# Low halves of weights by a negated cast on ScalarE and an adding transfer, and block sums on VectorE, in a hybrid encoder layer

## The chip, the core and the metric

The kernel is one launch on one core of one Trainium2 chip. It is written in a tile framework: the program allots named tiles from pools, and a scheduler sets the order of each engine's instructions and puts semaphore waits where a tile is not yet written or not yet free. The metric is the device time in microseconds, the median of the runs. Lower is better.

The engines are TensorE (PE, matmuls, with weight loads shown apart as PEld), VectorE (DVE), ScalarE (ACT), GpSimd (POOL) and SyncE (SP). SP and POOL also issue the transfers (DMA); in the code `dma` goes to SP's queue and `gdma` to POOL's.

## The reference

One layer for 1024 prompt tokens and 32 sample tokens, so T = 1056 columns, with D = 1024 and a feed-forward width of 2816. Everything is float32. Cut to what matters here:

```python
h = rms_norm(x, g_pre_mix)
z = h @ w_in                                    # split into q, k, v, HGRN2 inputs, gates ga and gb
ya = sink_attention(...)                        # windowed attention, 16 heads
yb = rms_norm(hgrn2(...), g) * silu(ob)         # gated linear recurrence, 8 heads
mix = sigmoid(ga) * (ya @ w_br_a) + sigmoid(gb) * (yb @ w_br_b)
x = x + rms_norm(mix @ w_out, g_post_mix)
hf = rms_norm(x, g_pre_ffn)
a, u = split(hf @ w_up, 2)                      # two halves of 2816 columns
a = causal_conv3(concat(prev, a)) + b_conv
x = x + rms_norm((gelu(a) * u) @ w_down, g_post_ffn)
x = x + (pe @ w_ple) * sigmoid(x @ w_ple_gate)
```

The outputs are x of both groups, the last keys and values, the recurrence's state and the convolution's tail.

## The kernel before, in words

**Split products.** A float32 product is made of three matmuls on a reduced type (fp32r). Each operand is split into a high half, hi = cast(raw), and a low half, lo = raw - hi. `product` adds hi x hi, hi x lo and lo x hi; the weight's low half is read by the third matmul only (L202, in the up stage L1867).

**Plain weights.** `plan` lists the weight tiles (128 columns, 512 KB) in the order of use. `next_w` returns the next one and calls `load_next` for the two behind it. `load_next` takes a raw tile ("wr", 2 buffers, loaded from DRAM by SP) and two of the eight 4 KB slots of the pool "wb" for hi and lo. hi comes from ScalarE (L181) and lo from VectorE (L184). The plan's entries 26 to 41 (n_first is 22) are the 8 tiles of w_br_a and the 8 of w_br_b. In this branch stage each tile meets four groups of 264 columns. A block of 24 matmuls fills one of six accumulator banks ("mm"), VectorE combines it with a gate tile "ta" (4 buffers), and POOL's queue stores the result to the DRAM tile mx_d (L1381).

**The up products.** A unit u is 128 columns of a with the 128 columns of u that belong to them, and there are 22 units. A unit is computed by a scheme of seven products (as Strassen and Winograd have it) in place of eight: its weights are seen as 2 x 2 blocks a11, a12, a21, a22 of 128 x 512 numbers, and the seven weight parts are

- part 0: a11
- part 1: a11 + s1, with s1 = a21 + a22
- part 2: a12
- part 3: a21 + a11, part 4: s1, part 5: a22
- part 6: a12 + a11 + s1

`unit_parts` is a generator that makes one part at each step: a cast to hi on ScalarE (L1625), the subtraction for lo on VectorE (L1626), both into one slot of "wb" (tile "wt"). The four block sums (L1632, L1633, L1634, L1639) are made on VectorE for unit 0 and on GpSimd (POOL) for the others. Three of them overwrite raw blocks, and s1 has a tile of its own, "sa", in a slot of "wb" too. `prepare` calls the generator so that parts stand three products ahead of their use (AHEAD = 3), so that a unit's first parts are made while the unit ahead is computed. The raw tiles (two of 512 KB a unit, loaded by SP at L1615) lie in "wr" for even units and in "wx" for odd ones, and the loads of unit u + 1 are written into the code behind part 3 of unit u.

Unit 0 is split early, in the z products' stage (`early_parts`), and its parts pass through the DRAM tiles pw_d.

**What follows a product.** `up_unit` runs the seven products of a unit, 24 matmuls each (2 column halves x 4 row blocks x 3); products 0 to 6 go to three accumulator tiles X, Y, Z ("st", 3 buffers). `after` takes them out: product 0 by ScalarE's copy to s1c (L1876), product 1 by VectorE's U2 = s1c - Y (L1878); L1894 is the last product's. Product 3 writes into Y again, so it waits for U2. At the unit's end `ff_tail` does the convolution: ScalarE's first tap (L1814), VectorE's other two (L1815, L1816), the gelu, and the product with u. The scheduler puts these beside the next unit's products.

Of the kernel before, what the change touches and what calls it, by code (L numbers as in the profile page):

```python
# [10 lines left out]
F32 = mybir.dt.float32  # L11
# [3 lines left out]
ALU = mybir.AluOpType  # L15
AX = mybir.AxisListType

P = 128
# [41 lines left out]
def layer_kernel(  # L60
# [10 lines left out]
    wp = ctx.enter_context(tc.tile_pool(name="wp", bufs=1, side="left"))  # L71
# [6 lines left out]
    def nm(s):  # L78
        n_names[0] += 1
        return f"{s}_{n_names[0]}"  # L80
# [4 lines left out]
    dma, gdma = nc.sync.dma_start, nc.gpsimd.dma_start  # L85
    V, S, G, E = nc.vector, nc.scalar, nc.gpsimd, nc.tensor
# [50 lines left out]
    def rows_cols(src, r0, c, n, kt):  # L137
        return src[0, r0:r0 + kt * P, c:c + n].rearrange("(k p) c -> p k c", p=P), kt, n
# [15 lines left out]
    n_first = len(plan)  # L154
# [11 lines left out]
    raws, ready, used = [], [], [0]  # L166

    def load_raw(raw=None):
        src, kt, n = plan[len(raws)]
        raws.append(raw or wp.tile([P, kt, n], F32, tag="wr", name=nm("wr"), bufs=2))  # L170
        dma(raws[-1][:], src)

    def load_next():
        _, kt, n = plan[len(ready)]
        if len(raws) == len(ready):
            load_raw()
        raw = raws[len(ready)]
        hi = wp.tile([P, kt, n], F32R, tag="wb", name=nm("wh"), bufs=8)
        lo = wp.tile([P, kt, n], F32R, tag="wb", name=nm("wl"), bufs=8)
        if hi_on[0] == "act":  # L180
            S.copy(hi[:], raw[:])  # L181
        else:
            V.tensor_copy(hi[:], raw[:])
        V.tensor_tensor(lo[:], raw[:], hi[:].bitcast(F32), op=ALU.subtract)  # L184
        ready.append((hi, lo))

    hi_on = ["act"]

    def next_w(ahead=2):
        while len(ready) < min(limit[0], used[0] + 1 + ahead):  # L190
            load_next()
        used[0] += 1
        return ready[used[0] - 1]
# [44 lines left out]
    def tr_bank():  # L238
        return bank(pp, "tr", 2)
# [738 lines left out]
    with right("bp") as bp:  # L978
# [322 lines left out]
        def more():  # L1301
            limit[0] = n_mix
            load_next()
# [10 lines left out]
        for c in range(4, 8):  # L1314
            u = unit(gate_out(tb_d[c]))
# [7 lines left out]
    def page(pool, n, shape, name):  # L1323

        return pool.tile(shape, F32R, tag=f"pg{n}", name=nm(name))
# [282 lines left out]
    raw_w, ready_w = {}, []  # L1608

    def unit_raw(u):  # L1610
        pool, tag = (wp, "wr") if u % 2 == 0 else (fp, "wx")
        t = []
        for h in (0, DFF):
            t.append(pool.tile([P, KT, P], F32, tag=tag, name=nm("wu"), bufs=2))
            dma(t[-1][:], rows_cols(w_up, 0, h + u * P, P, KT)[0])  # L1615
        raw_w[u] = t

    def unit_parts(u, s1, place, out):

        f1, f2 = raw_w.pop(u)  # L1620
        a11, a12, a21, a22 = f1[:, 0:4, :], f1[:, 4:8, :], f2[:, 0:4, :], f2[:, 4:8, :]

        def parts(i, src):
            t = place(i)
            S.copy(t[:, 0], src)  # L1625
            V.tensor_tensor(t[:, 1], src, t[:, 0].bitcast(F32), op=ALU.subtract)  # L1626
            out(i, t)

        adder = V if u < 1 else G

        parts(0, a11)
        adder.tensor_tensor(s1, a21, a22, op=ALU.add)  # L1632
        adder.tensor_tensor(a21, a11, a21, op=ALU.add)  # L1633
        adder.tensor_tensor(a11, a11, s1, op=ALU.add)  # L1634
        yield
        parts(1, a11)
        yield
        parts(2, a12)
        adder.tensor_tensor(a12, a12, a11, op=ALU.add)  # L1639
        yield  # L1640
        for i, src in enumerate((a21, s1, a22, a12)):
            parts(3 + i, src)
            yield

# [3 lines left out]
    def early_parts():  # L1648

        rw = page(lq, 4, [P, 2, KT, P], "rw")  # L1650
        rs_ = page(lq, 5, [P, 2, 2, 512], "rs")
        bufs = [page(lq, 6 + i, [P, 2, 2, 4, P], "pw") for i in range(2)]
        raw_w[0] = [rw[:, i].bitcast(F32) for i in range(2)]
        for i in range(2):
            dma(raw_w[0][i], rows_cols(w_up, 0, DFF * i, P, KT)[0])
        for i in range(2):
            dma(rs_[:, i].bitcast(F32), rows_cols(w_ple, 0, 512 * i, 512, 2)[0])

        place = [bufs[0][:, 0], bufs[0][:, 1], bufs[1][:, 0]]

        def store(i, t):
            gdma(pw_d[i][:], t.rearrange("p a k c -> p (a k c)").bitcast(F32))

        yield from unit_parts(0, bufs[1][:, 1, 0].bitcast(F32), lambda i: place[i % 3], store)
        for i in range(2):
            src = rs_[:, i].rearrange("p k c -> p (k c)")
            hi, lo = (place[(7 + 2 * i + a) % 3].rearrange("p a k c -> p (a k c)") for a in range(2))
            S.copy(hi, src.bitcast(F32))
            gdma(pw_d[7 + 2 * i][:], hi.bitcast(F32))
            V.tensor_tensor(lo, src.bitcast(F32), hi.bitcast(F32), op=ALU.subtract)  # L1670
            gdma(pw_d[8 + 2 * i][:], lo.bitcast(F32))
            yield
# [14 lines left out]
    n_parts, gens = [7], {}  # L1687

    def prepare(n):

        while n_parts[0] < min(n + 1, 7 * NF):
            u, i = divmod(n_parts[0], 7)
            if i == 0:
                if u not in raw_w:
                    unit_raw(u)
                s1 = wp.tile([P, 4, P], F32, tag="wb", name=nm("sa"), bufs=8)[:]
                gens[u] = unit_parts(u, s1, part_tile, lambda i, t: ready_w.append(t))
            next(gens[u])
# [43 lines left out]
    t = tr_bank()  # L1742
# [401 lines left out]
```

## Time and profile before

| | |
|---|---|
| median of 3 runs | 2002.01 us (2001.38 to 2003.11) |
| profiled execution | 2002.58 us |
| its span, first to last instruction | 2000.8 us |
| granted TensorE clock | 1.000 |
| PE busy | 1984.3 us (99%) |
| VectorE busy | 1424.5 us (71%) |
| ScalarE busy | 965.4 us (48%) |
| GpSimd busy | 228.4 us (11%) |

Times in rows of the profile are microseconds from the span's start. A row of a timeline gives start, length, engine, line, operation, result and inputs, partitions x elements, how many run together (x3), and in brackets how long the engine had been idle and which instruction released it. A row of a group has the count, the busy sum and the mean in nanoseconds of one, and then the idle time ahead of the group, by what ended it. A row of transfers has the count, the size of one, and the time from issue to landing. The branch stage lies around 940 us; the up products run from 1183 to 1637 us.

### The profile page before, as it was taken

Reading aid. Unit: us, or ns where it says so; the run is one execution under the profiler, and the core shown is the slowest. Engines: PE = TensorE matmul, PEld = TensorE weight load, DVE = VectorE, ACT = ScalarE, POOL = GpSimd, SP = SyncE. Lnnn points to the kernel's source line nnn. Section 1 sums busy time; section 2 is a strip of 40 time slices with the busy share of each in tenths; the row PEclk is TensorE's granted clock in tenths of the full one; section 3 lists DMA queues with packets and bytes.
Section 4 is the critical chain, followed back from the end, with each engine's and each line's share of the span. In section 5 each row is a group of like instructions: output and inputs, shape, how many; then the busy total and the mean of one; then the engine's idle time right before and its main releaser. Section 6 shows DMA issues by size and latency. Waiting matters only on the chain.

```text
span 2000.8 us, 37359 instructions
## 1 busy us (share of the span) xinstructions
PE 1984.3 (99%) x14304; PEld 1955.0 (98%) x14304; DVE 1424.5 (71%) x3138; ACT 965.4 (48%) x2159; POOL 228.4 (11%) x323
## 2 busy tenths in 40 slices
PE   8999999999999999999999999999999999999998
PEld 7899999999999999999999999999999999999998
DVE  6788888688888888554455788788888784655552
ACT  7555566566666666442124663333333344444432
POOL 1110100000000000002001023333333210000000
PEclk9999999999999999999999999999999999999999
DMA  7622311411111111377558582222222245655543
GB/s 257 155 92 85 106 53 55 154 43 58 58 37 51 41 54 54 123 241 220 166 165 291 173 288 70 80 76 86 76 86 76 86 141 195 213 192 173 171 130 80
DMA packets 253639, 247.47 MB, mean 124 GB/s; under 512 B 13893, under 2 KB 221912, under 8 KB 253461
## 3 DMA queue, kind: packets, MB, share of 16 engines
q1 hardware_dynamic: 245141, 218.59, 35.3%
q0 software_dynamic: 8240, 26.44, 3.7%
q8 instruction: 112, 1.84, 0.4%
q14 instruction: 66, 0.54, 0.1%
q10 hardware_dynamic: 80, 0.07, 0.0%
HBM read 177.56 MB, written 65.32 MB: 121 GB/s over the span
## 4 chain that ended last, share of the span: by engine, by line
PE 92%; DVE 4%; ACT 2%; DMA 1%; issue 1%; POOL 0%; SPq 0%; DVEq 0%; ACTq 0%; POOLq 0%
PE mm L200 14%; PE mm L201 14%; PE mm L202 14%; PE st L1867 7%; PE st L1866 7%; PE st L1865 7%; PE G L1009 2%; PE Y L1006 2%; PE G L1008 2%; PE G L1006 2%; PE Y L1009 2%; PE Y L1008 2%; PE tr L478 1%; PE X L1006 1%; PE so L1200 1%; PE X L1009 1%
## 5 line engine op out<-in xcount | busy, mean ns | idle before, releaser
L1865 PE MATMUL st<-op,wt 128*128 128x264 f32 x1232 | 348.6, 283 | 2.0 <-DVE Sp L1878 1.3
L1867 PE MATMUL st<-op,wt 128*128 128x264 f32 x1232 | 349.8, 284 | 0.0
L1866 PE MATMUL st<-op,wt 128*128 128x264 f32 x1232 | 347.6, 282 | 0.0
L184 DVE TENSOR_TENSOR wl<-wr,wh 128x1024 fp32r<-128x1024 f32 x129 | 157.9, 1224 | 120.7 <-ACT wh L181 111.7
L1865 PEld LDWEIGHTS st<-op,wt 128*128 128x128 f32 x1232 | 231.2, 188 | 3.5 <-DVE Sp L1878 1.7
L1866 PEld LDWEIGHTS st<-op,wt 128*128 128x128 f32 x1232 | 231.4, 188 | 0.0
L1867 PEld LDWEIGHTS st<-op,wt 128*128 128x128 f32 x1232 | 230.9, 187 | 0.0
L181 ACT CAST wh<-wr 128x1024 fp32r<-128x1024 f32 x116 | 121.8, 1050 | 197.7 <-PE mm L201 136.1
L200 PE MATMUL mm<-La,wh 128*128 128x384 f32 (+1 forms) x528 | 174.4, 331 | 0.0
L201 PE MATMUL mm<-Lb,wh 128*128 128x384 f32 (+1 forms) x528 | 170.9, 324 | 0.6 <-DVE Lb L710 0.6
L200 PE MATMUL mm<-ac,wh 128*128 128x352 f32 x528 | 170.8, 323 | 0.0
L202 PE MATMUL mm<-La,wl 128*128 128x384 f32 (+1 forms) x528 | 170.5, 323 | 0.2 <-DVE wl L685 0.2
L202 PE MATMUL mm<-ac,wl 128*128 128x352 f32 x528 | 169.8, 322 | 0.0
L201 PE MATMUL mm<-ac,wh 128*128 128x352 f32 x528 | 169.3, 321 | 0.0
L1625 ACT CAST wt<-wu 128x512 fp32r<-128x512 f32 x126 | 77.9, 619 | 186.6 <-POOL ab L1851 88.3
L200 PE MATMUL mm<-Ra,wh 128*128 128x264 f32 x512 | 145.4, 284 | 0.0
L201 PE MATMUL mm<-Rb,wh 128*128 128x264 f32 x512 | 145.0, 283 | 0.0
L202 PE MATMUL mm<-Ra,wl 128*128 128x264 f32 x512 | 145.0, 283 | 0.0
L1626 DVE TENSOR_TENSOR wt<-wu,wt 128x512 fp32r<-128x512 f32 x126 | 103.0, 820 | 39.0 <-ACT wt L1625 39.0
L462 ACT ACTIVATE sc<-sc,st 128x257 f32<-128x257 f32 (+1 forms) x144 | 69.7, 485 | 74.0 <-DVE st L457 73.0
L201 PEld LDWEIGHTS mm<-Lb,wh 128*128 128x128 f32 x528 | 99.4, 188 | 1.7 <-DVE Lb L710 1.4
L202 PEld LDWEIGHTS mm<-La,wl 128*128 128x128 f32 x528 | 99.2, 188 | 0.7 <-DVE wl L685 0.5
(496 smaller groups left out, 5694.8 us busy)
## 6 DMA issues: line engine op xcount, KB each, us to landing
wr<-in_w_down_dram SPq DMA_DIRECT2D x66, 512.0 KB
wu<-in_w_up_dram SPq DMA_DIRECT2D x42, 512.0 KB
wu<-in_w_in_dram SPq DMA_DIRECT2D x32, 512.0 KB
wr<-in_w_in_dram SPq DMA_DIRECT2D x25, 512.0 KB
ac<-act_d SPq DMA_DIRECT2D x66, 176.0 KB
act_d<-Up SPq DMA_DIRECT2D x21, 528.0 KB
wr<-in_w_out_dram SPq DMA_DIRECT2D x16, 512.0 KB
pw_d<-pw POOLq DMA_DIRECT2D x11, 512.0 KB, 5.6
```

The source lines that it names most:

```text
L181: S.copy(hi[:], raw[:])
L184: V.tensor_tensor(lo[:], raw[:], hi[:].bitcast(F32), op=ALU.subtract)
L200: E.matmul(ps, wh, a, start=first and n == 0, stop=False)
L201: E.matmul(ps, wh, b, start=False, stop=False)
L202: E.matmul(ps, wl, a, start=False, stop=last and n == len(ks) - 1)
L1006: E.matmul(o, wh, x[0][k], start=first and k == 0, stop=False, skip_group_check=True)
L1008: E.matmul(o, wh, x[1][k], start=False, stop=False, skip_group_check=True)
L1009: E.matmul(o, wl, x[0][k], start=False, stop=k == 3, skip_group_check=True)
L1626: V.tensor_tensor(t[:, 1], src, t[:, 0].bitcast(F32), op=ALU.subtract)
L1865: E.matmul(o, wh, xh, start=first and k == 0, stop=False, skip_group_check=True)
L1866: E.matmul(o, wh, xl, start=False, stop=False, skip_group_check=True)
L1867: E.matmul(o, wl, xh, start=False, stop=k == 3, skip_group_check=True)
```

## The change

Three things change.

1. For the plan's entries 26 to 41 (the branch weights), lo is no longer made by VectorE. ScalarE writes -raw into the lo tile (a negated cast), and a transfer of GpSimd's queue adds raw to it.

2. The same for the seven parts of each unit from 1 on. Unit 0 keeps VectorE's subtraction.

3. The four block sums of every unit are made on VectorE, and a11 + s1 goes to a new second half of the tile "sa", where before it overwrote a11. The last sum now goes into a11.

As written, the result of the adding transfer is -cast(raw) + raw, since the tile that ScalarE writes holds the reduced type.

```diff
@@ load_next
+        if n_first + 4 <= len(ready) < n_first + 20:
             S.copy(hi[:], raw[:])
+            S.mul(lo[:], raw[:], -1.0)
+            gdma(lo[:], raw[:], accum_op=ALU.add)
         else:
-            V.tensor_copy(hi[:], raw[:])
-        V.tensor_tensor(lo[:], raw[:], hi[:].bitcast(F32), op=ALU.subtract)
+            if hi_on[0] == "act":
+                S.copy(hi[:], raw[:])
+            else:
+                V.tensor_copy(hi[:], raw[:])
+            V.tensor_tensor(lo[:], raw[:], hi[:].bitcast(F32), op=ALU.subtract)
@@ unit_parts
-    def unit_parts(u, s1, place, out):
+    def unit_parts(u, s1, s2, place, out):
...
             S.copy(t[:, 0], src)
-            V.tensor_tensor(t[:, 1], src, t[:, 0].bitcast(F32), op=ALU.subtract)
+            if u:
+                S.mul(t[:, 1], src, -1.0)
+                gdma(t[:, 1], src, accum_op=ALU.add)
+            else:
+                V.tensor_tensor(t[:, 1], src, t[:, 0].bitcast(F32), op=ALU.subtract)
             out(i, t)
 
-        adder = V if u < 1 else G
-
         parts(0, a11)
-        adder.tensor_tensor(s1, a21, a22, op=ALU.add)
-        adder.tensor_tensor(a21, a11, a21, op=ALU.add)
-        adder.tensor_tensor(a11, a11, s1, op=ALU.add)
+        V.tensor_tensor(s1, a21, a22, op=ALU.add)
+        V.tensor_tensor(a21, a11, a21, op=ALU.add)
+        V.tensor_tensor(s2, a11, s1, op=ALU.add)
         yield
-        parts(1, a11)
+        parts(1, s2)
         yield
         parts(2, a12)
-        adder.tensor_tensor(a12, a12, a11, op=ALU.add)
+        V.tensor_tensor(a11, a12, s2, op=ALU.add)
         yield
-        for i, src in enumerate((a21, s1, a22, a12)):
+        for i, src in enumerate((a21, s1, a22, a11)):
             parts(3 + i, src)
             yield
@@ prepare
-                s1 = wp.tile([P, 4, P], F32, tag="wb", name=nm("sa"), bufs=8)[:]
-                gens[u] = unit_parts(u, s1, part_tile, lambda i, t: ready_w.append(t))
+                sa = wp.tile([P, 2, 4, P], F32, tag="wb", name=nm("sa"), bufs=8)
+                gens[u] = unit_parts(u, sa[:, 0], sa[:, 1], part_tile, lambda i, t: ready_w.append(t))
```

`early_parts` passes the second half of its scratch tile for s2. Lines of the changed file lie 5 higher in its first part and 8 higher from the up products on: L1814, L1815, L1816, L1876, L1878 of before are L1822, L1823, L1824, L1884, L1886 after, and the sums are L1639, L1640, L1641, L1646.

The scheduler orders the changed program anew. The next rows are VectorE's, before, from the last product of one unit (L1894) to U2 of the next (L1878) in a steady stretch of the up stage. The number behind a tile's name tells which allotment it is; `st` are accumulators, `ab` the convolution's input, `a` its sum, `Sp` holds s1c and U2, and a wait on PE, Activation or DMAHW is one on TensorE, ScalarE or a transfer of SP's queue.

```order
L1894 TENSOR_TENSOR Sp_14910<-Sp_14910,st_15645 128x528 [waits PE_49]
L1626 TENSOR_TENSOR wt_15990<-wu_15876,wt_15990 128x512 [waits DMAHW4_49,Activation_49]
L1898 TENSOR_TENSOR ab_15646<-Sp_14910,rbT 128x2x232 [waits DVE_49]
L1901 TENSOR_TENSOR ab_15646<-Sp_14910,rbT 128x32 x2
L1810 COPY tails<-ab_15646 128x2 [waits DVE_49]
L1811 COPY tails<-ab_15646 128x2 [waits DVE_49]
L1813 COPY ab_15646<-cach 128x2
L1815 TENSOR_SCALAR a_15856<-ab_15646,cvec,a_15856 128x1058 [waits Activation_49]
L1816 TENSOR_SCALAR a_15856<-ab_15646,cvec,a_15856 128x1058 [waits DVE_49]
L1878 TENSOR_TENSOR Sp_14910<-Sp_14910,st_15869 128x528 [waits PE_49,Activation_49]
```

The same stretch after; DMASW is a transfer of GpSimd's queue.

```order
L1902 TENSOR_TENSOR Sp_14926<-Sp_14926,st_15910 128x528 [waits PE_49]
L1906 TENSOR_TENSOR ab_15911<-Sp_14926,rbT 128x2x232 [waits DVE_49]
L1909 TENSOR_TENSOR ab_15911<-Sp_14926,rbT 128x32 x2
L1818 COPY tails<-ab_15911 128x2 [waits DVE_49]
L1819 COPY tails<-ab_15911 128x2 [waits DVE_49]
L1821 COPY ab_15911<-cach 128x2
L1639 TENSOR_TENSOR sa_16265<-wu_16151 128x512 [waits DMASW6_49,DMAHW0_49,DMASW1_49,PE_49]
L1823 TENSOR_SCALAR a_16128<-ab_15911,cvec,a_16128 128x1058 [waits Activation_49]
L1640 TENSOR_TENSOR wu_16151<-wu_16149,wu_16151 128x512 [waits DMASW6_49,DMAHW7_49,DMASW2_49,DVE_49]
L1824 TENSOR_SCALAR a_16128<-ab_15911,cvec,a_16128 128x1058 [waits DVE_49]
L1886 TENSOR_TENSOR Sp_14926<-Sp_14926,st_16141 128x528 [waits PE_49,Activation_49]
```

The low half's subtraction is gone, and two block sums stand between, one ahead of the first convolution step and one between the two.

ScalarE in the same stretch before, from part 4's cast (of tile "sa") to the copy of s1c:

```order
L1625 COPY wt_16130<-sa_15989 128x512 [waits PE_49]
L1625 COPY wt_16158<-wu_15878 128x512 [waits DVE_49]
L1625 COPY wt_16186<-wu_15876 128x512 [waits PE_49,Pool_49]
L1625 COPY wt_16215<-wu_16101 128x512 [waits DMAHW7_49,PE_49]
L1814 ACTIVATE a_16081<-ab_15871,cvec 128x1058 [waits DVE_49]
L1876 COPY Sp_14910<-st_16093 128x528 [waits PE_49]
```

And after, where the ACTIVATE rows of L1632 are the negated casts:

```order
L1630 COPY wt_16178<-sa_16033 128x512 [waits PE_49]
L1632 ACTIVATE wt_16178<-sa_16033 128x512
L1630 COPY wt_16207<-wu_15919 128x512 [waits DMASW1_49,PE_49,Activation_49]
L1632 ACTIVATE wt_16207<-wu_15919 128x512
L1630 COPY wt_16236<-wu_15917 128x512 [waits DMASW4_49,DMASW7_49,DVE_49,Activation_49]
L1632 ACTIVATE wt_16236<-wu_15917 128x512
L1630 COPY wt_16266<-wu_16149 128x512 [waits DMAHW7_49,DMASW2_49,PE_49]
L1632 ACTIVATE wt_16266<-wu_16149 128x512
L1822 ACTIVATE a_16128<-ab_15911,cvec 128x1058 [waits DVE_49,Pool_49]
L1884 COPY Sp_14926<-st_16140 128x528 [waits PE_49]
```

Each part has a second operation on ScalarE, and part 6's cast (wt_16236) now waits for transfers of GpSimd's queue, where before it waited for PE and GpSimd. One of them, DMASW7, counts part 4's transfer out of the tile sa_16033, whose slot wt_16236 takes.

GpSimd in one unit before:

```order
L1632 TENSOR_TENSOR sa_15989<-wu_15878 128x512 [waits DMAHW5_49,DMAHW0_49,PE_49]
L1633 TENSOR_TENSOR wu_15878<-wu_15876,wu_15878 128x512 [waits DMAHW4_49,Pool_49]
L1634 TENSOR_TENSOR wu_15876<-wu_15876,sa_15989 128x512 [waits DVE_49,Pool_49]
L1851 MEMSET ab_16096 128x2 [waits DVE_49,Activation_49]
L1639 TENSOR_TENSOR wu_15876<-wu_15876 128x512 [waits DVE_49,Pool_49]
```

And after:

```order
L1633 DMA wt_16034<-wu_15917 128x512 [waits DMASW3_49,DMAHW4_49,PE_49,Activation_49]
L1859 MEMSET ab_16143 128x2 [waits DVE_49,Activation_49]
L1633 DMA wt_16066<-sa_16033 128x512 [waits DVE_49,DMASW4_49,PE_49,Activation_49]
L1633 DMA wt_16095<-wu_15917 128x512 [waits DMASW6_49,PE_49,Activation_49]
L1633 DMA wt_16145<-wu_15919 128x512 [waits DMASW7_49,DMAHW5_49,PE_49,Activation_49]
L1633 DMA wt_16178<-sa_16033 128x512 [waits PE_49,Activation_49]
L1633 DMA wt_16207<-wu_15919 128x512 [waits DMASW1_49,PE_49,Activation_49]
L1633 DMA wt_16236<-wu_15917 128x512 [waits DMASW4_49,DMASW7_49,DVE_49,Activation_49]
```

The sums have left the queue and seven adding transfers, one for each part, have come in.

More of the change, by code (lines that the diff above doesn't have):

```diff
@@ L179, in load_next @@
         lo = wp.tile([P, kt, n], F32R, tag="wb", name=nm("wl"), bufs=8)
-        if hi_on[0] == "act":
+        if n_first + 4 <= len(ready) < n_first + 20:
             S.copy(hi[:], raw[:])
-        else:
-            V.tensor_copy(hi[:], raw[:])
-        V.tensor_tensor(lo[:], raw[:], hi[:].bitcast(F32), op=ALU.subtract)
+            S.mul(lo[:], raw[:], -1.0)
+            gdma(lo[:], raw[:], accum_op=ALU.add)
+        else:
+            if hi_on[0] == "act":
[3 more added lines that the diff above has]
+            V.tensor_tensor(lo[:], raw[:], hi[:].bitcast(F32), op=ALU.subtract)
         ready.append((hi, lo))
@@ L1662, in store @@
             gdma(pw_d[i][:], t.rearrange("p a k c -> p (a k c)").bitcast(F32))
-        yield from unit_parts(0, bufs[1][:, 1, 0].bitcast(F32), lambda i: place[i % 3], store)
+        yield from unit_parts(0, bufs[1][:, 1, 0].bitcast(F32), bufs[1][:, 1, 1].bitcast(F32),
+                              lambda i: place[i % 3], store)
         for i in range(2):
```

## The prediction

> **What bounds the kernel now.** I read the head of the page first, then the chain, then a table by stage, then the waits of TensorE alone.
>
> ```profile
> span 2000.8 us, 37359 instructions
> PE 1984.3 (99%) x14304; PEld 1955.0 (98%) x14304; DVE 1424.5 (71%) x3138; ACT 965.4 (48%) x2159; POOL 228.4 (11%) x323
> PE 92%; DVE 4%; ACT 2%; DMA 1%; issue 1%; POOL 0%; SPq 0%; DVEq 0%; ACTq 0%; POOLq 0%
> ```
>
> The matmul engine works in 1984.3 of 2000.8 us and carries 92% of the chain, so at most 16.5 us could be won by any edit that leaves the matmuls alone, as this one does. The next table has one row for each changed place: the branch products, the start of the up product, and its steady state.
>
> ```profile
> core 0: us, PE busy (x) PEld busy (x) DVE busy (x) ACT busy (x) POOL busy (x), PEclk, DMA share, GB/s
> 940.00:960.00 20.00, 20.00 (x167) 20.00 (x167) 5.45 (x9) 2.10 (x2) 3.75 (x7) 1.00 0.52 155
> 1206.00:1220.00 14.00, 12.63 (x100) 12.04 (x100) 13.97 (x21) 5.82 (x10) 7.15 (x4) 1.00 0.25 73
> 1300.00:1400.00 100.00, 100.00 (x828) 100.00 (x827) 80.56 (x119) 34.92 (x50) 33.30 (x26) 1.00 0.26 81
> ```
>
> In the steady state PE is busy for 100.00 of 100.00 us at full clock while VectorE, which the change relieves, is at 80.56. A unit is 7 products of 2 halves x 4 row blocks x 3 matmuls = 168 matmuls, and 828 take 100 us, so a unit takes 20.3 us (20.34 over many units) and a product 2.906. What PE does wait for in the changed places is three rows:
>
> ```profile
> 1203.36 0.39 PE L1865 MATMUL st<-op,wt 128*128 128x264 f32 x1 [0.20 <-DVE Sp L1878]
> 1206.76 0.39 PE L1865 MATMUL st<-op,wt 128*128 128x264 f32 x1 [0.21 <-DVE Sp L1883]
> 1218.59 0.39 PE L1865 MATMUL st<-op,wt 128*128 128x264 f32 x1 [1.06 <-DVE Sp L1878]
> ```
>
> Together 1.47 us, under 0.1% of the time. That is the ceiling of the gain, and the forecast turns on whether anything new gets in PE's way.
>
> **The work that moves.** These are the groups the change touches, and the nearest row of what it adds:
>
> ```profile
> L184 DVE TENSOR_TENSOR wl<-wr,wh 128x1024 fp32r<-128x1024 f32 x129 | 157.9, 1224 | 120.7 <-ACT wh L181 111.7 <-PE mm L202 5.2 <-issue 1.1
> L181 ACT CAST wh<-wr 128x1024 fp32r<-128x1024 f32 x116 | 121.8, 1050 | 197.7 <-PE mm L201 136.1 <-DMA wr<-in_w_down_dram 31.4 <-DMA wr<-in_w_out_dram 4.3
> L1626 DVE TENSOR_TENSOR wt<-wu,wt 128x512 fp32r<-128x512 f32 x126 | 103.0, 820 | 39.0 <-ACT wt L1625 39.0
> L1625 ACT CAST wt<-wu 128x512 fp32r<-128x512 f32 x126 | 77.9, 619 | 186.6 <-POOL ab L1851 88.3 <-PE st L1867 68.2 <-DVE wt L1626 22.9
> L1634 POOL TENSOR_TENSOR wu<-wu,sa 128x512 f32<-128x512 f32 x21 | 45.1, 2148 | 4.6 <-DVE wt L1626 3.1
> L1633 POOL TENSOR_TENSOR wu<-wu,wu 128x512 f32<-128x512 f32 x21 | 44.7, 2131 | 1.6
> L1632 POOL TENSOR_TENSOR sa<-wu 128x512 f32<-128x512 f32 x21 | 27.6, 1316 | 177.2 <-PE st L1867 172.3 <-DMA wu<-in_w_up_dram 4.9
> L1639 POOL TENSOR_TENSOR wu<-wu 128x512 f32<-128x512 f32 x21 | 27.2, 1293 | 87.3 <-DVE wt L1626 87.3
> ```
>
> VectorE loses 16 x 1.224 = 19.6 us in the branch stage and 147 x 0.82 = 120.5 us in the up stage (21 units of 7 parts), and takes over 84 block sums. ScalarE gains 16 x 1.05 = 16.8 and 147 x 0.62 = 91 us, the negated cast priced as the cast it repeats. GpSimd loses 45.1 + 44.7 + 27.6 + 27.2 = 144.6 us and issues 163 transfers more. A sum on VectorE I take at 0.69, as the subtractions of its 128x528 tiles that stand below, so 58 us (bounds 0.69 and 0.82). All of this lies beside PE, and what counts is order and arrival.
>
> **Part 1: VectorE's deadline within a unit.** Product 3 of a unit writes the accumulator bank that U2 = s1c - Y reads (L1878, in the changed file L1886). A steady unit on VectorE, and the same two lines at a place where GpSimd computes no sums:
>
> ```profile
> 1413.65 0.70 DVE L1894 TENSOR_TENSOR Sp<-Sp,st 128x528 f32<-128x528 f32 x1 [0.34 <-PE st L1867]
> ...
> 1417.37 1.64 DVE L1815 SCALAR_TENSOR_TENSOR a<-ab,cvec,a 128x1058 f32<-128x1058 f32 x1 [1.34 <-ACT a L1814]
> 1419.05 2.23 DVE L1816 SCALAR_TENSOR_TENSOR a<-ab,cvec,a 128x1058 f32<-128x1058 f32 x1
> 1421.20 0.69 DVE L1878 TENSOR_TENSOR Sp<-Sp,st 128x528 f32<-128x528 f32 x1
> ...
> 1644.26 1.32 DVE L1815 SCALAR_TENSOR_TENSOR a<-ab,cvec,a 128x1058 f32<-128x1058 f32 x1 [1.34 <-ACT a L1814]
> 1646.83 1.31 DVE L1816 SCALAR_TENSOR_TENSOR a<-ab,cvec,a 128x1058 f32<-128x1058 f32 x1
> ```
>
> The unit's last product ends when L1894 starts, 1413.65, so product 3 of the next begins at 1413.65 + 3 x 2.906 = 1422.37. L1878 now ends at 1421.89, 0.48 us before. In the changed order a block sum (L1640) comes between the two convolution steps ahead of it: 1417.37 + 1.32 + 0.69 + 1.31 + 0.69 = 1421.38, 0.99 us before, if the two steps run at 1.32 and 1.31 with GpSimd's sums gone. If they stay at 1.64 and 2.23, it ends at 1422.62 and each of 20 units pays 0.25 us: +5. I take the short values, since GpSimd then computes nothing.
>
> **Part 2: ScalarE's new wait.** In the changed order, part 6's cast takes the slot of the unit's own tile of sums, so it waits until part 4's adding transfer, which reads that tile, has landed. Until now nothing there waited for a transfer of the same unit. Behind that cast in ScalarE's queue stand part 6's negation, both operations of the next unit's part 0, the convolution's first step (L1814) and the copy of s1c. For the two convolution steps and U2, VectorE waits.
>
> ```profile
> 1407.84 0.62 ACT L1625 CAST wt<-sa 128x512 fp32r<-128x512 f32 x1 [2.29 <-PE st L1867]
> 1410.80 0.62 ACT L1625 CAST wt<-wu 128x512 fp32r<-128x512 f32 x1 [0.64 <-PE st L1867]
> 1413.65 0.62 ACT L1625 CAST wt<-wu 128x512 fp32r<-128x512 f32 x1 [2.23 <-PE st L1867]
> 1416.06 1.28 ACT L1814 ACTIVATE a<-ab,cvec 128x1058 f32<-128x1058 f32 x1 [1.79 <-DVE ab L1813]
> ```
>
> Part 4's cast of the unit after starts at 1407.84 + 20.34 = 1428.18, its negation ends at 1429.42, and its transfer lands a time L later. Then come 2 x 1.24 on ScalarE, 1.28 for L1814, and 1.32 + 0.69 + 1.31 + 0.69 on VectorE: 7.77 us. The deadline is 1422.37 + 20.34 = 1442.71, so L may be 5.52 us. Each microsecond beyond it costs 20 units a microsecond each (the first of the 21 is part 5), and from L = 5.7 that is 4 us. L stands in no row, because no transfer here adds. The nearest:
>
> ```profile
> t_d<-hs POOLq DMA_DIRECT2D x16, 192.0 KB, 2.3
> mx_d<-ta POOLq DMA_DIRECT2D x32, 132.0 KB, 3.6
> x<-xt_d POOLq DMA_DIRECT2D x8, 528.0 KB, 6.6
> pw_d<-pw POOLq DMA_DIRECT2D x11, 512.0 KB, 5.6
> DMA to landing us min/median/max: 3.6/5.6/9.1
> ```
>
> The last row belongs to the pw_d group. One adding transfer is 128 x 512 x 4 bytes = 256 KB. If the addition were free, L would lie between the 192 KB row and the fastest 512 KB one, 2.3 + (64/320) x (3.6 - 2.3) = 2.6, the lower bound. The upper bound is the slowest 512 KB row, 9.1, which would cost 20 x (9.1 - 5.5) = 72 us. I take 3.6, as if the destination were a second 256 KB to read in an engine group three quarters idle (0.26 above); half the pw_d rows, though, are at 5.6 or more, on the limit.
>
> The Trainium skill ("Collectives: The Full Stack", The bandwidth ceiling: the fold count and why AG ≠ RS ≠ AR) says that an adding copy reads two sources through the same read ring and so delivers about half the rate of a plain one, while the addition itself costs nothing. By it L is that of a 512 KB row: no loss at the fastest, 3.6, and 20 x 0.1 = 2 us at the median, 5.6. No run here shows it yet.
>
> **Part 3: what the transfers take of the DMA engines.** Seven times 262144 bytes in 20.34 us is 90 GB/s. The window's plain traffic used a share of 0.26 for 81 GB/s, so 0.29 more as a copy, 0.55 together, and 0.84 if each byte counts twice. Only above a factor of 2.55 do the engines fill; at 3 the share is 1.13, 2.65 us a unit. I take no loss, the bounds being 0 and 20 x 2.65 = 53 us.
>
> **Part 4: raw weights, issues, and when a low half is needed.** The raw loads two units ahead now wait for the last transfers that read the tile they replace.
>
> ```profile
> 1410.95 1.59 SPq L1615 DMA_DIRECT2D wu<-in_w_up_dram  x2
> L1381 POOL DMA_DIRECT2D mx_d<-ta x32 | 17.3, 539 | 592.3 <-DVE ta L1380 592.3
> ```
>
> Part 0 of the unit they serve is cast at 1413.65 + 20.34 = 1434.0, 23 us after the issue, so even a delay by 9.1 leaves 14. An issue keeps GpSimd for 0.54 us, 7 x 0.54 = 3.8 us of each 20.34, in place of 144.6/21 = 6.9 us of sums. Parts are prepared about three products ahead and more, and only the third matmul of each group of three reads the low half: part 1's, cast near 1422, is used at 1413.65 + 20.34 + 2.906 = 1436.9. All cost nothing; the cover is the three products of lead, at least 8.7 us, gone only when L nears that.
>
> **Part 5: the first units.** The 1.06 us at 1218.59 come from a queue on VectorE:
>
> ```profile
> 1202.27 0.69 DVE L1626 TENSOR_TENSOR wt<-wu,wt 128x512 fp32r<-128x512 f32 x1
> ...
> 1211.76 0.60 ACT L1876 COPY Sp<-st 128x528 f32<-128x528 f32 x1 [0.80 <-PE st L1867]
> 1213.70 2.98 DVE L1626 TENSOR_TENSOR wt<-wu,wt 128x512 fp32r<-128x512 f32 x3
> 1217.84 0.69 DVE L1878 TENSOR_TENSOR Sp<-Sp,st 128x528 f32<-128x528 f32 x1
> ```
>
> Three subtractions of low halves (2.98) stood ahead of L1878. They go, and one or two block sums come in (1.4 at most), so L1886 ends by about 1217.84 + 0.69 - 2.98 + 1.4 = 1217.0, before the 1218.59 - 1.06 = 1217.53 at which PE stood ready: a gain of 1.06. The first product of unit 1 ended near 1211.7 (the copy released by PE). Its second part is cast after the sums that follow the subtraction at 1202.27: 1202.27 + 3 x 0.69 + 2 x 0.62 = 1205.6, so L up to 6.1 does no harm there. The other two waits (0.20, 0.21) belong to unit 0 and stay.
>
> **Part 6: the branch stage.** Sixteen low halves of 512 KB come by transfer, two to three weights ahead:
>
> ```profile
> 941.24 1.05 ACT L181 CAST wh<-wr 128x1024 fp32r<-128x1024 f32 x1 [10.55 <-PE mm L201]
> ```
>
> The cast waited 10.55 us for PE to free its slot, and ScalarE works 2.10 of 20 us in that window. A weight lasts 96 matmuls, 11.5 us at that window's 167 in 20.00, so a transfer of 9.1 lands well within the two weights of lead. On GpSimd's queue the issue stands between two stores of results (mx_d), which can only be late by the negation's end, some 2 us (2 x 1.05), less than a block of 24 matmuls (2.9). I take 0; bounds 0 and 16 x 1 us if every weight held the stores up by a microsecond that reached PE.
>
> **Sum.** 0 - 1.06 + 0 + 0 = -1.06 us. The profiled execution took 2002.58 us (its span 2000.8 and 1.78 around it), 0.57 above the median of the runs, 2002.01; so 2001.5 on its scale and 2001.0 on the median's. Its own range is 2000.0 to 2004.0: the whole 1.47 and a little won, or the 2 us lost at a median L of 5.6.
>
> **The rivals.**
> - Slower by ScalarE's wait (part 2): the mechanism is the slot that part 6 shares with the sums, the price 20 us for each microsecond of L above 5.5, and it decides at 5.7. For it: the 512 KB median of 5.6 and maximum of 9.1. Against it: a quarter-loaded DMA, and the pw_d rows write to DRAM, which these transfers do not. At L = 6.5, 2001.0 + 20 = 2021.
> - Slower by full DMA engines (part 3): an adding byte costs three plain ones. For it: no row shows an addition at all. Against it: the factor must pass 2.55. At 3: 2001 + 53 = 2054.
> - Slower by VectorE's steps that stay long (part 1), 2001 + 5 = 2006. For it: no row shows why they are longer beside the sums. Against it: 1.32 and 1.31 where there are none.
> - Slower in the branch stage (part 6), 2001 + 16 = 2017. Against it: 10.55 us of idle time ahead of the cast.
> - Faster by over 4 us: PE would have to lose waits outside the changed places, of which the chain shows none that this touches.
>
> **How the numbers follow.** A difference of 0.2%, 4 us, is about what a measurement of this kernel can tell from none. Chances: forecast 0.60; ScalarE's wait 0.24, since half of the nearest rows sit at the limit but the idle DMA speaks for the fast half; full engines 0.07; long steps 0.04; branch stage 0.03; faster 0.02. So faster 0.02, same 0.60, slower 0.38. The range begins at 2000.0; its top, 2030, takes in ScalarE's wait up to L = 5.5 + 29/20 = 6.95 and leaves out the full engines and the third of that rival above (0.08), with the 0.02 below some 0.17.
>
> **What would show it.** Right: no wait of PE over 0.3 us in the up stage after 1220, DMA share 0.5 to 0.85 there, landings of the 256 KB transfers at 3 to 5.5 us, VectorE down by about 80 us, ScalarE up by about 108, L1823 and L1824 at 1.3. Wrong: in every unit a wait of PE for L1886, with part 6's cast on ScalarE waiting for a transfer (part 2), PE waiting for a low half's transfer at a share near 1 (part 3), or PE waiting for L1886 with L1823 and L1824 at 1.6 and 2.2 (part 1).

## The result and the profile after

The changed kernel takes 2006.54 us (median of 13 runs, 2003.77 to 2011.33) against 2001.6 before: a ratio of 1.0025, 95% interval [1.0017, 1.0034], so it is slower by 0.25%. The profiled execution has a span of 2005.8 us. This is the head of its page and its chain by engine:

```profile
span 2005.8 us, 37906 instructions
PE 1985.8 (99%) x14304; PEld 1956.6 (98%) x14304; DVE 1325.7 (66%) x3059; ACT 1056.1 (53%) x2322; POOL 223.4 (11%) x402
PE 93%; DMA 3%; ACT 2%; DVE 1%; issue 1%; POOL 0%; SPq 0%; ACTq 0%; DVEq 0%; POOLq 0%
```

VectorE is 98.8 us lighter and ScalarE 90.7 heavier, as the change wants, and PE has the same matmuls. But the chain now has 3% of DMA where it had 1%, and the list of PE's waits has a new head:

```profile
engine line waited for: us in total, times, longest us
PE mm L205 <- DVE ta L1385: 4.8, 2, 2.8
PE tr L678 <- POOL ident masks.py:199: 2.5, 1, 2.5
PE st L1873 <- DVE Sp L1891: 1.1, 1, 1.1
```

The second row was there before. The third, in the up stage, takes the place of the 1.06 us at 1218.59. The first is new, and it lies in the branch stage, where nobody waited before: L205 is the first matmul of a block, L1385 VectorE's product of an accumulator bank with the gate tile. The up stage does not lose. Its first and last matmuls of L1865 start at 1183.2 and 1636.9 before; those of L1873 now start at 1190.0 and 1642.5, 6.8 and 5.6 us later. So the up stage won 1.2 us, and the stages ahead of it lost 6.8. The stretch where they lost it, before and then after, in the table of windows (PE, PEld, DVE, ACT, POOL busy, clock, DMA share, GB/s):

```profile
900.00:910.00 10.00, 10.00 (x85) 10.00 (x85) 6.26 (x14) 4.87 (x11) 1.62 (x3) 1.00 0.96 292
910.00:920.00 10.00, 10.00 (x85) 10.00 (x84) 5.09 (x11) 4.40 (x8) 2.04 (x4) 1.00 0.75 229
920.00:930.00 10.00, 10.00 (x85) 10.00 (x84) 3.19 (x6) 0.36 (x1) 2.81 (x6) 1.00 0.73 222
```

```profile
900.00:910.00 10.00, 8.96 (x75) 8.75 (x73) 4.01 (x12) 3.24 (x10) 1.65 (x3) 1.00 0.93 265
910.00:920.00 10.00, 6.36 (x48) 5.94 (x48) 4.21 (x12) 4.71 (x10) 1.97 (x3) 1.00 1.02 280
920.00:930.00 10.00, 9.82 (x69) 9.82 (x70) 2.83 (x8) 5.46 (x8) 3.04 (x5) 0.83 0.89 242
```

The DMA engines were at 0.96, 0.75 and 0.73 here before the change, not at the 0.52 of the window around 950 on which the forecast rested. (The stage's first matmul is at 871.56, well ahead of the 940 us at which the overview puts it.) PE's two waits in the changed kernel's timeline:

```profile
910.91 0.39 PE L205 MATMUL mm<-Ra,wh 128*128 128x264 f32 x1 [1.94 <-DVE ta L1385]
920.18 0.59 PE L205 MATMUL mm<-Ra,wh 128*128 128x264 f32 x1 [2.82 <-DVE ta L1385]
```

**How close it stood before.** A block is 24 matmuls. The 32 blocks of w_br_a, the stage's first half, start their matmuls from 871.6 to 964.0 before, so a block takes 2.90 us. There are six banks, so block k needs the bank that VectorE emptied for block k - 6. The first block starts at 871.56 before and at 871.1 after. In VectorE's timeline, counted from the stage's first row, these are row 1 and row 11 of before (the closest of them), and then row 1 and row 8 of after:

```profile
877.65 0.42 DVE L1380 SCALAR_TENSOR_TENSOR ta<-ta,mm 128x264 f32<-128x264 f32 x1
...
914.54 0.42 DVE L1380 SCALAR_TENSOR_TENSOR ta<-ta,mm 128x264 f32<-128x264 f32 x1
```

```profile
885.04 0.43 DVE L1385 SCALAR_TENSOR_TENSOR ta<-ta,mm 128x264 f32<-128x264 f32 x1 [3.19 <-DMA ta<-ta_d]
...
910.43 0.42 DVE L1385 SCALAR_TENSOR_TENSOR ta<-ta,mm 128x264 f32<-128x264 f32 x1
```

Before, row 11 frees its bank at 914.96, and the block six later (the seventeenth) is due at 871.56 + 16 x 2.90 = 918.0: 3.0 us to spare, in a stretch where the list of PE's waits shows nothing. After, the first row comes 7.4 us later than before and waits for a gate tile's load, and row 8 frees its bank at 910.85 where the fourteenth block was due at 871.1 + 13 x 2.90 = 908.8: 2.0 us too late, against the wait of 1.94 in the row above.

What held row 8 stands ahead of it in VectorE's queue: five splits of the second branch's input (Yb), which wait for ScalarE's casts, which wait for loads (ld) of yb_d:

```profile
907.97 2.08 ACT L228 CAST Ya<-ld 128x264 fp32r<-128x264 f32 x5 [6.45 <-DMA ld<-yb_d]
```

```profile
908.41 2.11 DVE L229 TENSOR_TENSOR Yb<-ld,Ya 128x264 fp32r<-128x264 f32 x5 [5.88 <-ACT Ya L228]
```

These loads were issued from 900.83 on, just after the adding transfer that GpSimd issued at 899.67. SyncE was held up as well, 1.9 us for that transfer to land, ahead of the raw weight's load at 907.31; the loads that held row 8 had gone out before, so PE's first wait does not come from this hold. What it adds to the second wait is not separated here.

### The profile page after: what moved, and what is told of

Its sections match the earlier page's. It is cut to its first block, busy times and chain, and to the rows that moved or that the text cites. A ratio compares the mean times of both kernels' runs of the same rounds, so it can differ in the third digit from the quotient of the medians.

```text
span 2005.8 us, 37906 instructions
## 1 busy us (share of the span) xinstructions
PE 1985.8 (99%) x14304; PEld 1956.6 (98%) x14304; DVE 1325.7 (66%) x3059; ACT 1056.1 (53%) x2322; POOL 223.4 (11%) x402
## 4 chain that ended last, share of the span: by engine, by line
PE 93%; DMA 3%; ACT 2%; DVE 1%; issue 1%; POOL 0%; SPq 0%; ACTq 0%; DVEq 0%; POOLq 0%
PE mm L205 14%; PE mm L206 14%; PE mm L207 13%; PE st L1875 7%; PE st L1873 7%; PE st L1874 7%; PE G L1014 2%; PE Y L1011 2%; PE G L1013 2%; PE G L1011 2%; PE Y L1014 2%; PE Y L1013 2%; PE tr L483 1%; PE X L1011 1%; PE Z L1014 1%
## 5 line engine op out<-in xcount | busy, mean ns | idle before, releaser
L1873 PE MATMUL st<-op,wt 128*128 128x264 f32 x1232 | 348.3, 283 | 1.6 <-DVE Sp L1891 1.1
L1873 PEld LDWEIGHTS st<-op,wt 128*128 128x128 f32 x1232 | 231.2, 188 | 2.5 <-DVE Sp L1891 1.3
L189 DVE TENSOR_TENSOR wl<-wr,wh 128x1024 fp32r<-128x1024 f32 x113 | 138.3, 1224 | 105.7 <-ACT wh L186 97.3
L186 ACT CAST wh<-wr 128x1024 fp32r<-128x1024 f32 x100 | 105.1, 1051 | 136.9 <-PE mm L206 86.3
L205 PE MATMUL mm<-La,wh 128*128 128x384 f32 (+1 forms) x528 | 174.5, 331 | 0.0
L205 PE MATMUL mm<-ac,wh 128*128 128x352 f32 x528 | 170.6, 323 | 0.0
L205 PE MATMUL mm<-Ra,wh 128*128 128x264 f32 x512 | 146.5, 286 | 4.9 <-DVE ta L1385 4.8
L1630 ACT CAST wt<-wu 128x512 fp32r<-128x512 f32 x105 | 64.5, 614 | 84.5 <-issue 39.6
L1633 POOL DMA_DIRECT2D wt<-wu x105 | 89.1, 851 | 121.1 <-ACT wt L1632 95.1
L205 PEld LDWEIGHTS mm<-Ra,wh 128*128 128x128 f32 x512 | 97.1, 190 | 5.5 <-DVE ta L1385 5.5
```

Of the source, the lines that this page charges most:

```text
L205: E.matmul(ps, wh, a, start=first and n == 0, stop=False)
L1633: gdma(t[:, 1], src, accum_op=ALU.add)
L1873: E.matmul(o, wh, xh, start=first and k == 0, stop=False, skip_group_check=True)
```

## The experiments

The theory: the adding transfers of the branch weights add load to DMA engines that are already full when that stage begins (Ya and Yb, gates and weights are read back at the same time). Loads that VectorE needs then land later, and the six banks no longer cover it. The rivals: the up stage's transfers or ScalarE's wait there; or the branch weights' longer way itself (two operations on ScalarE, a transfer in GpSimd's queue, the raw tile held until the landing).

**One half of the change at a time.** For the first kernel the branch weights go back to VectorE:

```diff
-        if n_first + 4 <= len(ready) < n_first + 20:
+        if False:
             S.copy(hi[:], raw[:])
```

> The branch weights' low halves go back to VectorE; the up stage stays as changed. Theory (the branch stage's start is too full for the transfers): the loss goes and the up stage's gain of about 0.9 us stays, so 2000.7 against 2001.6 before, PE with no wait over 0.3 us between 870 and 970, share of the DMA engines still near 0.83 in the up stage. Rival (the seven adding transfers a unit, or their wait on ScalarE, cost something): 2005 to 2007.

Measured: 2000.96 us, ratio 0.9996 [0.9987, 1.0005]. The loss is gone. PE's longest wait in the up stage is 0.86, and the share of DMA there is 0.81.

The second kernel is the one before with the changed `load_next` alone:

```diff
+        if n_first + 4 <= len(ready) < n_first + 20:
             S.copy(hi[:], raw[:])
+            S.mul(lo[:], raw[:], -1.0)
+            gdma(lo[:], raw[:], accum_op=ALU.add)
```

> The up stage goes back to VectorE's subtractions and GpSimd's sums; only the sixteen branch weights use the negated cast and the adding transfer. Theory: the whole loss, 2006.5 + 0.9 = 2007.4, with 4 to 5 us of PE's waits for VectorE's gate product between 900 and 925. Rival (the loss is the up stage's): 2001.6.

Measured: 2007.11 us, 1.0026 [1.0017, 1.0035]. The whole loss is the branch stage's. PE's waits for L1385 were 2.6 us here, with 0.9 for a weight's cast, less than foretold; the stage's first half, from its first to its last matmul, takes 97.0 us (872.5 to 969.5) where it took 92.4 before.

**Which of the sixteen weights.** The range of entries is cut to the first six, then to the last ten:

```diff
-        if n_first + 4 <= len(ready) < n_first + 20:
+        if n_first + 4 <= len(ready) < n_first + 10:
```

> Only the first six branch weights use the transfer (830 to 912 us in the changed kernel's trace), the other ten VectorE. Theory (what counts is the crowded start, where the tiles ya and yb are read back too): the whole loss stays, 2006 to 2007. Rival (every one of the sixteen weights costs its share by its longer way): 2000.7 + 6/16 x 5.8 = 2002.9.

```diff
-        if n_first + 4 <= len(ready) < n_first + 20:
+        if n_first + 10 <= len(ready) < n_first + 20:
```

> The first six branch weights go back to VectorE, the other ten use the transfer. Theory: no loss, 2000.7, although ten adding transfers are left in the branch stage. Rival (each weight its share): 2000.7 + 10/16 x 5.8 = 2004.3.

Measured: 2006.1 us, 1.0023 [1.0014, 1.0031], with the first six alone; 2001.31, 0.9996 [0.9988, 1.0005], without them. It is not a price for each weight. Ten transfers later in the same stage cost nothing, and six at its start cost everything. First the wait of PE with the first six, then the windows without them:

```profile
PE mm L205 <- DVE ta L1385: 2.6, 2, 2.4
```

```profile
900.00:910.00 10.00, 10.00 (x85) 10.00 (x84) 6.24 (x15) 4.85 (x11) 1.66 (x4) 1.00 1.02 315
910.00:920.00 10.00, 10.00 (x85) 10.00 (x84) 3.67 (x11) 3.16 (x7) 1.08 (x2) 1.00 0.72 211
920.00:930.00 10.00, 10.00 (x85) 10.00 (x85) 1.64 (x5) 3.01 (x4) 3.08 (x5) 1.00 0.83 222
```

Without the first six PE is busy throughout, even with the engines full for ten microseconds, so a share near 1 is not enough by itself: what counts is whether a bank comes free in time. The reckoning of blocks and banks holds here too. With the first six, row 8 frees its bank 2.5 us late (912.48 against 872.3 + 13 x 2.90), and PE waited 2.39; without them, row 11 is the closest, at 918.21 against 872.6 + 16 x 2.90 = 919.0. That is only 0.8 us to spare in the profiled execution, so the ten cost nothing by a small margin.

**Bytes or the longer way.** VectorE makes the branch weights' low halves again, and GpSimd's queue carries transfers that nothing waits for:

```diff
+    dm = [dp.tile([P, 1024], F32, name=f"dm{i}") for i in range(2)]
...
             V.tensor_tensor(lo[:], raw[:], hi[:].bitcast(F32), op=ALU.subtract)
+        if n_first <= len(ready) < n_first + 2:
+            gdma(dm[len(ready) % 2][:], lo[:].rearrange("p k c -> p (k c)").bitcast(F32))
+        elif n_first + 4 <= len(ready) < n_first + 20:
+            gdma(dm[len(ready) % 2][:], lo[:].rearrange("p k c -> p (k c)").bitcast(F32), accum_op=ALU.add)
```

> VectorE makes the branch weights' low halves as before; beside that, GpSimd's queue adds each finished low half (512 KB) to a spare DRAM tile that nobody reads. Nothing of the kernel's own work waits for it and no raw tile is held longer. Up stage as changed. Theory B (the bytes alone crowd the DMA engines): most of the loss is there, 2004 to 2007. Theory W (the longer way of the low half and the raw tile that comes free later, with SyncE's queue held up behind it): 2000.7 to 2001.5.

Then with `raw` in place of `lo` as the source of the added sixteen:

> The same, but the spare tile has the raw weight added, so that the raw tile comes free only when that transfer has landed, as in the change. Theory B: as with the low half as source, 2004 to 2007. Theory W: the loss comes with the raw tile, 2004 to 2007 here and about 2001 there.

Measured: 2011.22 us, 1.0051 [1.0037, 1.0065], and 2011.17, 1.0044 [1.0032, 1.0057]. The added transfers alone are enough to cost as much, and holding the raw tile until the landing adds nothing to be seen (five runs of each). The loss is larger than the change's. These transfers go to DRAM and land in 7.3 and 5.8 us (median) where the change's take 5.6, and PE's waits are not all the same ones: in the first kernel 2.3 us for casts of the first branch's input (Ra) and 1.3 for the gate product, in the second 5.2 for the gate product. So they show that load suffices and don't measure the change's share of it.

In the next kernel the order and the waits are the change's, and only the addition is gone:

```diff
-            gdma(lo[:], raw[:], accum_op=ALU.add)
+            gdma(lo[:].bitcast(F32), raw[:])
```

> In the changed kernel the sixteen transfers of the branch stage copy the raw weight and add nothing, so the low half there is the raw weight (the branch products come out wrong); order, waits and places are those of the change, and so is the up stage. Theory B with a byte of an adding transfer counted twice: half the extra load, so less than half the loss, 2001 to 2003.5. Theory W, or an addition that costs no more than a copy: 2006.5.

Measured: 2002.3 us, 1.0005 [0.9996, 1.0014]: nearly the whole loss goes with the addition, though the transfers, the issues and the negated casts are still there. One wait of 2.0 us for L1385 is left in its profile, so it stands just at the edge. The plain transfer also lands sooner, so this kernel separates the addition from the rest and not the load from the landing. The two transfers, adding and plain, in the lists of transfers:

```profile
wl<-wr POOLq DMA_DIRECT2D x16, 512.0 KB, 5.6
```

```profile
wl<-wr POOLq DMA_DIRECT2D x16, 512.0 KB, 3.9
```

**What an addition costs the DMA engines.** The same edit in the up stage's parts, with the branch weights on VectorE:

```diff
-                gdma(t[:, 1], src, accum_op=ALU.add)
+                gdma(t[:, 1].bitcast(F32), src)
```

> Branch weights by VectorE; in the up stage the seven transfers of each unit from 1 on copy the raw part and add nothing (the up products come out wrong), all waits and places as in the change. The prediction's estimate for a copy: share of the DMA engines 0.26 + 0.29 = 0.55 in the steady stretch, where the adding transfers had 0.82. If an addition costs no more than a copy: 0.82 again. Time 2001 either way, since TensorE waits for none of them.

Measured: 1999.3 us, 0.9987 [0.9976, 0.9997]. The steady stretch of the changed kernel, and of this one, in the table of windows:

```profile
1300.00:1600.00 300.00, 300.00 (x2480) 300.00 (x2479) 187.00 (x307) 156.57 (x250) 87.66 (x117) 1.00 0.82 171
```

```profile
1300.00:1600.00 300.00, 300.00 (x2479) 300.00 (x2478) 186.49 (x309) 157.41 (x250) 56.98 (x118) 1.00 0.51 170
```

Nearly the same bytes a second (the last column counts them once) keep the engines busy 0.82 of the time when they add and 0.51 when they copy. Over the 0.26 of the kernel before that is 0.56 against 0.25, a factor of 2.2 for an added byte. The landing takes 2.6 us as a copy (256 KB, median) and 4.1 as an addition.

**ScalarE's wait for part 4.** The chain of the prediction's part 2 stayed hidden in the change, so it was stretched:

```diff
-                S.mul(t[:, 1], src, -1.0)
+                S.mul(t[:, 1], src, -2.0 if i == 4 else -1.0)
                 gdma(t[:, 1], src, accum_op=ALU.add)
+                if i == 4:
+                    gdma(t[:, 1], src, accum_op=ALU.add)
```

> In the changed kernel part 4 of each unit is negated twice over and raw is added by two transfers, one after the other (its low half comes out doubled, so the up products are wrong). In the changed kernel's trace part 6's cast on ScalarE begins 3.73 us after part 4's negation, ScalarE idles 0.67 us behind it, and U2 ends 1.45 us ahead of product 3, so 5.85 us are free. Theory of the prediction's part 2 (part 6 waits for part 4's landing, and each microsecond past the slack costs each unit one): two landings are 7.5 to 8.5, so 20 x 1.65 to 20 x 2.65 = 33 to 53 more than the changed kernel, 2040 to 2060, with a wait of TensorE for L1887 (U2) in every unit. Rival (parts are prepared early enough, no such chain): 2006.5.

Measured: 2033.39 us, 1.0159 [1.0145, 1.0173], 26.9 more than the change. One more transfer of 256 KB a unit costs 1.3 us a unit, with the DMA share at 0.83 where the change has 0.84. The chain is real. Its waits of PE's matmuls, and ScalarE's rows of one unit with that wait (L1824 is the convolution's first step, L1886 the copy of s1c):

```profile
PE st L1875 <- ACT Sp L1886: 11.5, 14, 2.7
PE st L1875 <- DVE Sp L1893: 2.6, 2, 2.1
PE st L1875 <- DVE Sp L1888: 1.1, 7, 0.2
```

```profile
1434.06 0.58 ACT L1886 COPY Sp<-st 128x528 f32<-128x528 f32 x1
...
1453.50 0.62 ACT L1630 CAST wt<-wu 128x512 fp32r<-128x512 f32 x1 [2.35 <-DMA wt<-sa]
1454.03 0.63 ACT L1632 ACTIVATE wt<-wu 128x512 fp32r<-128x512 f32 x1
1454.56 1.26 ACT L1824 ACTIVATE a<-ab,cvec 128x1058 f32<-128x1058 f32 x1
1455.73 0.57 ACT L1886 COPY Sp<-st 128x528 f32<-128x528 f32 x1
```

Part 6's cast waits for part 4's landing, and from one s1c copy to the next it is 21.67 us where a unit takes 20.34: 20 x 1.33 = 26.6. The matmuls' waits in the list are 15.2 us; the weight loads ahead of them (PEld) wait 25.2 (2.4 in the changed kernel), near the whole loss, 15.4 of it for the copy of s1c and 6.4 for U2. So PE waits above all for the copy of s1c, and less for U2: product 2 adds onto the bank X that the copy reads, and that comes one product earlier than the deadline that was reckoned with. The loss is below the 33 to 53 expected; in this kernel's order the next unit's part 0 stands ahead of part 6, so two operations fewer follow the wait. That makes for less, though no run takes it apart. Part 4's negation ended 8.2 us ahead of the cast.

**The sums.** They go back to GpSimd, with the up stage's transfers kept and the branch weights on VectorE (the other three sums likewise):

```diff
+        adder = G if u else V
         parts(0, a11)
-        V.tensor_tensor(s1, a21, a22, op=ALU.add)
+        adder.tensor_tensor(s1, a21, a22, op=ALU.add)
```

> Branch weights by VectorE; in the up stage the adding transfers stay and the four block sums go back to GpSimd. The prediction's reading of the two convolution steps (1.32 where GpSimd computes nothing, 1.64 and 2.23 beside its sums): they are long again, 1.6 and 2.1, and the sums 1.3 to 2.1, and the time stays within 1 us of 2001 since no sum stands between the steps. If something else made them long (the low halves on VectorE): 1.32 and 1.32.

Measured: 2017.26 us, 1.0074 [1.0057, 1.0091], where at most 1 us was expected. The steps are long again. The group of the first of them here, and then in the next kernel, where VectorE has the sums:

```profile
L1824 DVE SCALAR_TENSOR_TENSOR a<-ab,cvec,a 128x1058 f32<-128x1058 f32 x22 | 48.4, 2202 | 41.7 <-ACT a L1823 38.6 <-issue 3.1
```

```profile
L1823 DVE SCALAR_TENSOR_TENSOR a<-ab,cvec,a 128x1058 f32<-128x1058 f32 x22 | 29.1, 1321 | 4.8 <-ACT a L1822 4.8
```

That part of the expectation held. What it overlooked was ScalarE's wait for a landing out of the sums' tile: 40.7 us in 20 units, up to 5.7, where the changed kernel has 16.9 in 18. GpSimd's queue now holds four sums of 1.6 to 2.2 us beside the transfers, landings are 5.1 us (median), and with the long steps behind it U2 comes late: 8.8 us of PE's waits are for U2 (L1887 there), 4.5 for the copy of s1c.

Last, the third edit alone, with every low half by VectorE:

```diff
-            if u:
+            if False:
                 S.mul(t[:, 1], src, -1.0)
                 gdma(t[:, 1], src, accum_op=ALU.add)
```

> Only the third edit: the four block sums of every unit on VectorE with the new place for a11 + s1, and all low halves by VectorE as before, so no adding transfer at all. The prediction's part 1: the convolution steps take 1.32 and 1.31, the two sums ahead of U2 keep it about a microsecond ahead of product 3, and the time is 2000.7 to 2002. Rival (the sums need the transfers' relief on VectorE: with four sums more in a unit VectorE is the bound): above 2010.

Measured: 1999.7 us, 0.9989 [0.9979, 0.9999]. It is about 0.1% faster than the kernel before, at the edge of what can be told, and so clearly below the changed kernel. The steady stretch:

```profile
1300.00:1400.00 100.00, 100.00 (x828) 100.00 (x827) 82.77 (x139) 33.95 (x49) 0.50 (x5) 1.00 0.26 81
```

VectorE took over four sums a unit and is at 82.77 in place of 80.56, since its own steps became shorter: the two convolution steps 1.32 each in place of 1.60 and 2.13, the subtraction of a low half 0.69 in place of 0.82.

## Why the prediction was wrong

The forecast was 2001.0 and no change that can be told; it came out at 2006.54 and slower. The direction was missed. That the time lies in the range given is luck: the range reached up to 2030 for ScalarE's wait (part 2), which cost nothing here. The 2006 of the rival with the long convolution steps is met by chance as well, since the steps ran at 1.32.

- **Part 6, the branch stage, is the step that failed.** It priced the stage at 0 from a window and a cast at 940, seventy microseconds into it, and put at nothing what the sixteen transfers take from the other loads there. Between 900 and 930 the DMA engines stood at 0.73 to 0.96 before the change, and VectorE emptied a bank only 3.0 us before it was needed. The cover that the step named, two weights of lead, is that of the low halves, and it held: in the changed kernel PE never waited for one. What was late was other tiles' loads in the same engines, and by them the emptying of the banks. The part's own upper bound, the stores held up in GpSimd's queue, gave 2017 by the wrong mechanism: row 8's store was issued at 911.15, 0.30 us behind the row. The stage's first half runs 7.2 us longer from its first to its last matmul (871.6 to 964.0 before, 871.1 to 970.7 after): 4.8 of waits, about 1.3 of slow clock (below), and about 1 in single wider gaps between matmuls around the waits, such as 0.37 us at 914.18 where 0.12 is usual.
- **Part 3, the load of the transfers, had the right price in the wrong place.** Its 0.84 for bytes that count twice was measured as 0.82, and its 0.55 for a copy as 0.51; PE didn't mind in the up stage, as said. The same price applied to the branch stage's start (512 KB for each weight, on engines that were nearly full) would have given the warning, though not the size of the loss, which needs the banks' slack as well. By the rule quoted from the Trainium skill ("Collectives: The Full Stack", The bandwidth ceiling: the fold count and why AG ≠ RS ≠ AR), half the rate, the extra load is twice a copy's; the trace agrees roughly, with 2.2.
- **Part 1** was right: the steps run at 1.32 in all 22 units, and U2 stays ahead of product 3. Short steps came from the missing sums on GpSimd, as the kernel with the sums put back shows.
- **Part 2** was right that the coupling exists and stays hidden. The landings of all parts are 3.2 to 7.9 us, median 4.1; those out of the sums' tile (parts 1 and 4) have a median of 4.0, where 3.6 was taken for L against a slack put at 5.5. ScalarE waited for one in 18 units, 2.3 us at most, and PE has no wait for it in the steady stretch. That an excess costs every unit is borne out (1.33 a unit, 26.9 in all); the reader was above all s1c ahead of product 2.
- **Part 4** was right: SyncE waits 273.2 us between 1230 and 1620 for adding transfers to land before raw tiles are reloaded, and no wait of PE, VectorE or ScalarE in that stretch is for a raw tile's load. An issue of an adding transfer kept GpSimd 0.85 us where 0.54 was priced, and no wait of PE shows it.
- **Part 5** was half right. The wait of 1.06 went, and one of 1.13 came at 1229.97. On VectorE the last sum of the unit (L1646) overwrites a11 and so waits for a transfer that reads it, and the subtraction that PE needs stands behind it:

```profile
1228.61 0.69 DVE L1646 TENSOR_TENSOR wu<-wu,sa 128x512 f32<-128x512 f32 x1 [4.64 <-DMA wt<-wu]
1229.22 0.70 DVE L1891 TENSOR_TENSOR Sp<-st,Sp 128x528 f32<-128x528 f32 x1
```

The prediction had looked for such a wait on ScalarE and not on VectorE. In the kernel whose parts are copied plainly, with shorter landings, it is gone; its median is 1.7 us below that of the same kernel with the addition, which the intervals don't separate.

- ScalarE gained 90.7 us in place of 108: consecutive operations of 0.62 start 0.53 apart and overlap. VectorE lost 98.8 in place of 80, since its convolution steps grew shorter too.

## What to carry to other kernels

A transfer that takes work off an engine is paid for in DMA time, so look up the DMA share at each place where it will run, the most crowded window first, and count an adding transfer about twice. Where a stage's results leave through a ring of accumulator banks, work out how long before its reuse each bank is emptied: PE's list of waits was empty here with 3.0 us left. And take a change apart: the one edit of the three that may have helped, the block sums on VectorE (0.1%, at the edge of the measurement), was hidden by the one that hurt.

## What the runs showed of the hardware

- An adding transfer within the chip's buffers took 2.2 times the DMA time of a copy of the same bytes (a share of 0.56 against 0.25 above the other traffic), and landed in 4.1 us in place of 2.6 for 256 KB, 5.6 in place of 3.9 for 512 KB, each under its own kernel's load.
- GpSimd's own arithmetic slowed VectorE's here. The same convolution steps took 2.1 to 2.2 us beside four sums a unit on GpSimd (1.60 and 2.13 in the kernel before) and 1.32 without them, and the 128x512 subtraction 0.82 against 0.69.
- After the wait of 2.82 us at 920.18 matmuls start 0.22 us apart, for twelve or thirteen of them, where they start 0.12 apart otherwise; the granted clock from 920.2 to 924.2 is 0.60. The kernel with the first six transfers shows the same after 2.39 us, and the one that adds low halves to DRAM after two waits close together, of 0.65 and 1.70 us (0.50 from 891 to 893). The one that adds raw weights to DRAM does not after 2.52. The Trainium skill ("TensorE: Matmul & The Clock Gate", Part 1: The HAM clock gate (the "warmup" mystery)) has the throttle come after an idle window of about 3.4 us that runs freely; the waits here were all shorter than that, so the trace does not agree with 3.4 us as the least idle time that counts. Why one of them had no effect stays open.
